# Layer 1 of a two-layer block on Trainium2: the two heads' transposes and value products issued together, output parts split earlier, a third accumulator bank and a moved table load

## The chip, the cores and the metric

The kernel runs on one core of a Trainium2 chip. The time is the device time of one execution in microseconds (us). A core has TensorE (PE, matrix products, with its weight loads shown as PEld), VectorE (DVE), ScalarE (ACT), GpSimd (POOL) and SyncE (SP, which issues most of the DMAs here). Each engine works through its own list of instructions in order, and waits on semaphores for the others.

## What is computed

The reference is a first block (time mixing of eight heads by a recurrence, and eight heads of stick-breaking attention), followed by two layers on 512 tokens of width 1024 with 256 tokens of context: layer 0 with a short convolution and a gated FFN, layer 1 with neighbourhood attention of 16 heads of width 64 and the same kind of FFN. All of it is float32. The change lies in layer 1:

```python
q, k, v = _qkv_heads(h, w_qkv, g_q, g_k)          # q and k normalised per head
qc, kc, vc = _qkv_heads(hc, w_qkv, g_q, g_k)      # of the context
...
s_win = jnp.einsum('bqhd,brkhd->bhqrk', q_r, k_r) * scale + bias[None]
s_ctx = jnp.einsum('bqhd,bchd->bhqc', q_r, kc) * scale
s = jnp.concatenate([s_win.reshape(...), s_ctx], axis=-1)
p = jax.nn.softmax(s, axis=-1)
o = p_win @ v_r + p_ctx @ vc
...
x = x + g1 * (o @ w_out)
h = rms_norm(x, norm_ffn) * (1 + sc2) + sh2
gate, up = jnp.split(h @ w_in, 2, axis=-1)
x = x + g2 * ((silu(gate) * up) @ w_out)
```

## The kernel before, in words

Every float32 operand of a large product is split in two fp32r parts, hi (a cast on ScalarE) and lo (a subtraction on VectorE), and a product is three matmuls (`mm3`, L172 hi by hi, L173 lo by hi, L174 hi by lo). Weights come by DMA into `st` and are split by `split_w` (L155 cast, L156 subtraction) into four pairs of buffers `wh`, `wl` of 512 columns; one weight tile of 1024 columns takes two of them. Names ending in h and l (h0h, h0l) are such parts.

The order on each engine is set by a list scheduler at build time, from priorities and its estimates of durations. `order()` adds a dependency that the scheduler respects and that makes no semaphore.

PSUM banks are asked for by tag: `acc` (two banks), `cacc` (one), `sm` for scores, `pt` for transposes and head norms, `py` for a pair's output.

Layer 1 takes its 16 heads in eight pairs (`na_pair`, p = 0 to 7). A pair projects q and k (`xgemm`, and the context's k in `cacc`), normalises them per head (`hnorm`: L811 square, L298 and L299 block sums of `hsh` and `hsl`, L242 and L249 logarithm and exponential, L818, L819 and L821 the gain) and lays the two heads out in `qh`, `ql` and `kk` (L826, L827; L839, L840). GpSimd subtracts the bias from the mask (`bt`, L846). Then come four blocks of 128 queries, each with two heads e = 0, 1. For one head of one block: scores (L863, L864, two or four matmuls into `sm`), addition of mask and bias with a row minimum on VectorE (L868), exponential with row sum on ScalarE (L870), reciprocal on VectorE (L871), scaling on GpSimd (L872), four transposes of 128 columns in float32 on PE (L876 into `pT`), and a copy out of PSUM (L877, VectorE for e = 0, ScalarE for e = 1). After two blocks `na_values` issues ten value products (L896, five for each head, in float32; the two heads write different halves of the partitions of `py`); these two blocks are called a half here. The projections of the next pair are put by the scheduler between the scores, transposes and value products of this one, so PE has other work while a head's probabilities are made.

A pair's output is copied to a float32 tile `o{k}` (L882 on ScalarE, L883 on VectorE). After the loop over pairs in the program, each is split into `oh` parts (L307, L308), pair 7's straight from PSUM. The output product takes its eight tiles `attn_w_out[m]` one after the other through the two `acc` banks, each with eight steps k over the pairs. In the schedule its first tiles fill PE during pair 7, which has no next pair to project.

Then the FFN's norm: `rsqrt` (L242 logarithm, L249 exponential) and `modulate` (L288 on VectorE, L290 on ScalarE for h..h, L291 on VectorE for h..l), in two halves of 256 tokens. The first FFN tile (`lead`) runs gate and up together by halves; it holds both `acc` banks. The FFN's tile applies tanh to the gate (L643) and multiplies (L644), which frees the gate's bank, then takes up (L649) and splits the result (L307, L308). Tanh needs another set of function tables on ScalarE than logarithm and exponential in this kernel; the load is placed right ahead of the first tanh.

## Time and profile before

| what | value |
|---|---|
| runs | 2081.96, 2076.53, 2077.85 us; median 2077.85 us |
| profiled execution | 2080.14 us, of which the span from first to last instruction is 2078.4 us |
| mean granted TensorE clock | 0.994 |
| layer 1's attention, first score of pair 0 to last value product of pair 7 | 1440.34 to 1665.32 us |
| last matmul of the first FFN tile, first of the second | 1721.36 and 1724.59 us |

In the rows of the profile a group or an instruction is written as line, engine, operation, output <- inputs, partitions times elements. A row of the timeline begins with the start in us from the span's start and the duration; in brackets stands the engine's idle time before it and what ended it. Matmuls are pipelined: one of 512 columns is shown with some 0.39 us, while the next starts some 0.23 us after it, so spacing is read from starts. A clock (PEclk) of 1.00 is the full TensorE clock.

### The profile page before, as it was taken

To read this page: it belongs to the slowest core of one execution; us is meant where nothing else is said; L and a number is where in the kernel's file an instruction comes from. 1 tells how busy PE (TensorE), PEld (TensorE's weight loads), DVE (VectorE), ACT (ScalarE), POOL (GpSimd) and SP (SyncE) were. 2 spreads that over 40 slices of the span, in tenths; PEclk is the share of its full clock that TensorE was granted. 3 is DMA by queue.
4 is the path that set the end of the run, shared out by engine and by line. 5 is a ranking of instruction groups with operands and counts; after the bars stand their busy time and mean duration, and the time that the engine had idled before them with its cause. 6 is when DMAs were issued, how large, how long until landed. Compare 5 with 4: busy or idle time off the path is not lost.

```text
span 2078.4 us, 33492 instructions
## 1 busy us (share of the span) xinstructions
PE 2029.1 (98%) x13564; PEld 1637.2 (79%) x13564; DVE 1230.9 (59%) x2641; ACT 795.6 (38%) x1493; POOL 131.5 (6%) x212
## 2 busy tenths in 40 slices
PE   6999999998999999999999999999999999999999
PEld 3766667666888888888888888898777687888887
DVE  2869888658766738675446343444666754444443
ACT  3536444446322224221222222335776743323232
POOL 0000000000000000000001000001223200000000
PEclk9999999999999999999999999999999999999999
DMA  7432222122233312344235221122111122323323
GB/s 280 150 113 92 94 74 93 40 81 83 92 122 122 122 61 93 131 133 151 94 135 177 72 96 61 58 82 67 56 52 51 36 82 82 101 93 97 98 98 103
DMA packets 61355, 203.59 MB, mean 98 GB/s; under 512 B 6928, under 2 KB 8976, under 8 KB 61200
## 3 DMA queue, kind: packets, MB, share of 16 engines
q1 hardware_dynamic: 45360, 145.77, 21.6%
q0 software_dynamic: 15120, 55.06, 8.1%
q8 instruction: 106, 1.74, 0.4%
q10 hardware_dynamic: 720, 0.62, 0.1%
q14 instruction: 49, 0.40, 0.1%
HBM read 199.32 MB, written 2.10 MB: 97 GB/s over the span
## 4 chain that ended last, share of the span: by engine, by line
PE 87%; ACT 3%; DVE 3%; issue 1%; POOL 0%; DMA 0%; POOLq 0%; DVEq 0%; ACTq 0%
PE acc L173 20%; PE acc L174 20%; PE acc L172 19%; PE cacc L174 5%; PE cacc L173 5%; PE cacc L172 5%; PE py L896 2%; PE pT L876 1%; PE ss L1150 1%; PE so L1172 1%; PE sm L863 1%; PE sm L864 1%; PE G L980 1%; DVE nt L288 1%; PE ss L1165 1%
## 5 line engine op out<-in xcount | busy, mean ns | idle before, releaser
L155 ACT CAST wh<-st 128x512 fp32r<-128x512 f32 (+2 forms) x481 | 292.1, 609 | 722.0 <-PE acc L173 283.2
L156 DVE TENSOR_TENSOR wl<-st,wh 128x512 fp32r<-128x512 f32 (+2 forms) x481 | 323.4, 674 | 350.7 <-ACT wh L155 347.4
L172 PE MATMUL acc<-xzzh,wh 128*128 128x512 f32 x352 | 138.8, 394 | 0.0
L174 PE MATMUL acc<-xzzh,wl 128*128 128x512 f32 x352 | 138.0, 392 | 0.0
L173 PE MATMUL acc<-xzzl,wh 128*128 128x512 f32 x352 | 138.0, 392 | 0.0
L210 DVE CUSTOM_DVE_ANT_0 junk<-ast,cb,vec 128x512 bf16<-128x512 f32 x168 | 125.0, 744 | 15.7 <-DMA ast<-in_w_ada_dram 13.6
L210 DVE CUSTOM_DVE_ANT_0 junk<-ast,cb,m 128x512 bf16<-128x512 f32 x168 | 125.5, 747 | 2.8
L200 POOL DMA_DIRECT2D ast<-in_w_ada_dram x96 | 50.7, 528 | 996.5 <-DVE m L210 887.1
L174 PEld LDWEIGHTS acc<-xzzh,wl 128*128 128x128 f32 x352 | 66.0, 188 | 14.8
L173 PEld LDWEIGHTS acc<-xzzl,wh 128*128 128x128 f32 x352 | 66.1, 188 | 13.5 <-issue 0.5
L172 PEld LDWEIGHTS acc<-xzzh,wh 128*128 128x128 f32 x352 | 66.1, 188 | 13.4 <-issue 0.5
L173 PE MATMUL acc<-h7l,wh 128*128 128x512 f32 (+1 forms) x164 | 65.2, 397 | 4.1 <-DVE h7l L308 4.1
L172 PE MATMUL acc<-h0h,wh 128*128 128x512 f32 (+1 forms) x164 | 65.6, 400 | 3.0 <-DVE fs L644 3.0
L173 PE MATMUL cacc<-czzl,wh 128*128 128x256 f32 x240 | 68.1, 284 | 0.0
L172 PE MATMUL cacc<-czzh,wh 128*128 128x256 f32 x240 | 67.7, 282 | 0.0
L174 PE MATMUL cacc<-czzh,wl 128*128 128x256 f32 x240 | 67.3, 280 | 0.0
L172 PE MATMUL acc<-h3h,wh 128*128 128x512 f32 (+1 forms) x164 | 65.1, 399 | 0.9 <-DVE x L452 0.9
L174 PE MATMUL acc<-h2h,wl 128*128 128x512 f32 (+1 forms) x164 | 65.8, 401 | 0.0
L174 PE MATMUL acc<-h0h,wl 128*128 128x512 f32 (+1 forms) x164 | 65.7, 401 | 0.0
L173 PE MATMUL acc<-h3l,wh 128*128 128x512 f32 (+1 forms) x164 | 65.4, 399 | 0.3 <-DVE h3l L291 0.3
L174 PE MATMUL acc<-h7h,wl 128*128 128x512 f32 (+1 forms) x164 | 65.1, 397 | 0.4 <-issue 0.4
L173 PE MATMUL acc<-h5l,wh 128*128 128x512 f32 (+1 forms) x164 | 65.4, 399 | 0.0
(731 smaller groups left out, 5539.4 us busy)
## 6 DMA issues: line engine op xcount, KB each, us to landing
ast<-in_w_ada_dram POOLq DMA_DIRECT2D x96, 512.0 KB, 3.8
st<-in_ffn_w_in_dram SPq DMA_DIRECT2D x88, 512.0 KB, 3.5
st<-in_ffn_w_out_dram SPq DMA_DIRECT2D x32, 448.0 KB, 3.4
st<-in_w_in_dram SPq DMA_DIRECT2D x24, 512.0 KB, 3.5
st<-in_conv_w_in_dram SPq DMA_DIRECT2D x24, 512.0 KB, 3.5
ast<-in_ada_n_dram SPq DMA_DIRECT2D x16, 512.0 KB, 8.9
st<-in_ffn_w_out_dram SPq DMA_DIRECT2D x16, 512.0 KB, 3.5
st<-in_w_qk_dram SPq DMA_DIRECT2D x16, 512.0 KB, 3.4
```

The lines of the kernel that those rows point to most:

```text
L155: nc.scalar.copy(hi[:, :n], sl)
L156: nc.vector.tensor_tensor(lo[:, :n], sl, hi[:, :n].bitcast(F32), ALU.subtract)
L172: mm(out, lhsT=lh, rhs=rh, start=first, stop=False)
L173: mm(out, lhsT=lh, rhs=rl, start=False, stop=False)
L174: return mm(out, lhsT=ll, rhs=rh, start=False, stop=last)
L200: self.nc.gpsimd.dma_start(st, src)
L210: i = self.nc.vector.tensor_tensor_reduce(out=junk, in0=st[:, hs], in1=c[:, hs], scale=0.5, scalar=o if hf else self.V(bname, j), op0=ALU. ...
L288: nc.vector.scalar_tensor_tensor(t, xs[k], gain[:, k:k + 1], rstd, op0=ALU.mult, op1=ALU.mult)
L863: mm(o, lhsT=qh[:, e, qs], rhs=ks, start=True, stop=False)
L864: mm(o, lhsT=ql[:, e, qs], rhs=ks, start=False, stop=True)
L876: nc.tensor.transpose(pT[:, to], s[:, 128 * i:128 * i + 128], self.C("ident"))
L896: self.nc.tensor.matmul(po[r, cs], lhsT=v[:, r], rhs=pts[e][:, blk:blk + n].rearrange("p a t -> p (a t)"), start=i == 0, stop=i == len(wor ...
```

## The change

- `na_pair` first makes both heads' probabilities of a block, then issues both heads' transposes. The first head's transposes are ordered behind the second head's scaling, and in `na_values` the first head's products behind the last copy of the transposes. Both are orders for the scheduler, without a semaphore. (The second head's scaling is what `ready` names after the loop.)
- The outputs of pairs 0 to 3 are split straight from PSUM into tiles of their own (`o0h`, `o0l` and so on). Those of pairs 4 to 6 are copied as before and split when pair 7 is issued, pair 7's from PSUM.
- The output product's tile m = 2 and the gate of FFN tile i = 1 use the bank `cacc`, which is free by then, in place of `acc`.
- The load of the table set with tanh is placed behind the last exponential of the FFN's norm.

```diff
--- before.py
+++ after.py
@@ -554,8 +554,8 @@
                 nc.sync.dma_start(A["dbg_x0"][k], xs[k])
                 nc.sync.dma_start(A["dbg_c0"][k], self.xc[k])
 
-    def gemm2(self, src, h, hc, k0=0, k1=KT):
-        po = self.psum("acc")
+    def gemm2(self, src, h, hc, k0=0, k1=KT, tag="acc"):
+        po = self.psum(tag)
         w = self.load_w(src[:, k0 * 128:k1 * 128], (k1 - k0) * 128)
         outs = [(po, h)]
         if hc is not None:
@@ -636,7 +636,7 @@
             hid = []
             for i in range(t0, t0 + np_):
                 lead = i == 0 and self.lead((w1[0], w1[NH_T]), *hs, halves=split)
-                pg = lead[0] if lead else self.gemm2(w1[i], *hs)
+                pg = lead[0] if lead else self.gemm2(w1[i], *hs, tag="cacc" if split and i == 1 else "acc")
                 ss = []
                 for (_, _, n, pre, _), ps in zip(st, pg):
                     s = pool.tile([128, n], F32, tag=pre + "cs", name="fs")
@@ -679,8 +679,8 @@
             return pre[t]
         return self.xgemm(W[t], h)
 
-    def xgemm(self, src, h, k0=0, k1=KT):
-        out = self.psum("acc")
+    def xgemm(self, src, h, k0=0, k1=KT, tag="acc"):
+        out = self.psum(tag)
         self.gemm(out, src, dict((k0 + i, t) for i, t in enumerate(h)), k0, k1)
         return out
 
@@ -744,22 +744,27 @@
                 nc.scalar.copy(va[:, 2:4, cs], v2(pvs[1]))
                 for t in range(2):
                     nc.vector.tensor_copy(vc[4 * t + qd], pvs[2][:, 256 * t:256 * t + 256])
-            os = [pool.tile([128, S], F32, name=f"o{k}") for k in range(KT - 1)] + [None]
+            oh = [self.hl(pool, S, f"o{k}") for k in range(4)]
+            os = [pool.tile([128, S], F32, name=f"o{k}") for k in range(4, KT - 1)]
             wp = es.enter_context(self.open(name="naw", bufs=2))
             self.qls = [wp.tile([128, 2, S], F32R, name=f"ql{i}", bufs=1) for i in range(2)]
             for t in self.qls:
                 nc.gpsimd.memset(t[64:128, 0].bitcast(F32), 0.0)
                 nc.gpsimd.memset(t[0:64, 1].bitcast(F32), 0.0)
             for p in range(8):
-                last = self.na_pair(p, W, h, hc, gq, va, vc, mask, bts, os[p], wp)
-            oh = []
-            for k, tag in enumerate(("qh", "kk", "pt0", "pt1") * 2):
-                t = wp.tile([128, 2, S], F32R, tag=tag, name="oh", bufs=2)
-                oh.append((t[:, 0], t[:, 1]))
-                if k < KT - 1:
-                    self.split(oh[k], os[k])
-            for a, b in ((slice(0, 448), slice(64, S)), (slice(448, S), slice(0, 64))):
-                self.split((oh[7][0][:, a], oh[7][1][:, a]), last[:, b])
+                po = self.na_pair(p, W, h, hc, gq, va, vc, mask, bts, wp)
+                if 4 <= p < KT - 1:
+                    nc.scalar.copy(os[p - 4][:, :448], po[:, 64:])
+                    nc.vector.tensor_copy(os[p - 4][:, 448:], po[:, :64])
+                    continue
+                if p == KT - 1:
+                    for k, tag in enumerate(("qh", "kk", "pt0", "qh")):
+                        t = wp.tile([128, 2, S], F32R, tag=tag, name="oh", bufs=2)
+                        oh.append((t[:, 0], t[:, 1]))
+                        if k < 3:
+                            self.split(oh[4 + k], os[k])
+                for a, b in ((slice(0, 448), slice(64, S)), (slice(448, S), slice(0, 64))):
+                    self.split((oh[p][0][:, a], oh[p][1][:, a]), po[:, b])
             sx, late = {"bufs": 4, "acc_tag": "q", "sq_tag": "s"}, []
             rstd = wp.tile([128, S], F32, tag="q", name="rstd")
             hv = [slice(0, 256), slice(256, 512)]
@@ -770,7 +775,7 @@
                 self.stat(m, xs[m], S, wp, "x", sx, c)
 
             for m in range(6):
-                add(m, self.xgemm(A["attn_w_out"][m], oh), slice(0, S))
+                add(m, self.xgemm(A["attn_w_out"][m], oh, tag="cacc" if m == 2 else "acc"), slice(0, S))
             for m in (6, 7):
                 w, po = self.load_w(A["attn_w_out"][m], 1024), self.psum("acc")
                 self.gemm(po[:, hv[0]], None, cut(oh, hv[0]), w=w)
@@ -786,7 +791,8 @@
                 turn(0, range(2 * i, 2 * i + 2))
                 add(m, po, hv[1])
             self.prefetch(A["ffn_w_in1"][0], A["ffn_w_in1"][NH_T])
-            self.rsqrt(rstd[:, hv[1]], sx["ps"][:, hv[1]])
+            done = self.rsqrt(rstd[:, hv[1]], sx["ps"][:, hv[1]])
+            self.order(nc.scalar.preload_act_table_set("exp_and_others"), done)
             turn(0, range(4, KT))
             turn(1, range(KT))
             if self.dbg:
@@ -797,7 +803,7 @@
         for k in range(KT):
             nc.sync.dma_start(A["out"][k], xs[k])
 
-    def na_pair(self, p, W, h, hc, gq, va, vc, mask, bts, oh, wp):
+    def na_pair(self, p, W, h, hc, gq, va, vc, mask, bts, wp):
         nc = self.nc
         TT, STT = nc.vector.tensor_tensor, nc.vector.scalar_tensor_tensor
         mm = nc.tensor.matmul
@@ -850,6 +856,7 @@
             qs = slice(128 * j, 128 * j + 128)
             if j % 2 == 0:
                 pts = [wp.tile([128, 8, 128], F32, tag=f"pt{e}", name=f"pt{e}", bufs=2) for e in range(2)]
+            probs = []
             for e in range(2):
                 ps = self.psum("sm")
                 ke = kk[:, e]
@@ -869,20 +876,21 @@
                                                scalar=3.0e38, op0=ALU.add, op1=ALU.min, accum_out=st[:, 0:1])
                 nc.scalar.activation(s, s, AF.Exp, scale=-1.0, bias=st[:, 0:1], accum_out=st[:, 1:2])
                 nc.vector.reciprocal(st[:, 2:3], st[:, 1:2])
-                nc.gpsimd.tensor_scalar(s, s, st[:, 2:3], 1.0, op0=ALU.mult, op1=ALU.mult)
+                ready = nc.gpsimd.tensor_scalar(s, s, st[:, 2:3], 1.0, op0=ALU.mult, op1=ALU.mult)
+                probs.append(s)
+            for e, s in enumerate(probs):
                 pT = self.psum("pt", (128, 4, 128), "pT")
                 for i in range(4):
                     to = 1 - i if j == 3 and i < 2 else i
-                    nc.tensor.transpose(pT[:, to], s[:, 128 * i:128 * i + 128], self.C("ident"))
-                (nc.scalar.copy if e else nc.vector.tensor_copy)(pts[e][:, j % 2::2], pT)
+                    t = nc.tensor.transpose(pT[:, to], s[:, 128 * i:128 * i + 128], self.C("ident"))
+                    if e == 0:
+                        self.order(t, ready)
+                copied = (nc.scalar.copy if e else nc.vector.tensor_copy)(pts[e][:, j % 2::2], pT)
             if j % 2:
-                self.na_values(p, j // 2, po, pts, va, vc)
-        if oh is None:
-            return po
-        nc.scalar.copy(oh[:, :448], po[:, 64:])
-        nc.vector.tensor_copy(oh[:, 448:], po[:, :64])
-
-    def na_values(self, p, half, po, pts, va, vc):
+                self.na_values(p, j // 2, po, pts, va, vc, copied)
+        return po
+
+    def na_values(self, p, half, po, pts, va, vc, ready):
         c0 = 256 * half
         near = va[:, :, 128 * p:128 * p + 128]
         far = [vc[4 * n + p // 2][:, 128 * (p % 2):128 * (p % 2) + 128] for n in range(2)]
@@ -893,9 +901,11 @@
             for e in range(2):
                 r = slice(64 * e, 64 * e + 64)
                 cs = slice(c0 + 128 * col, c0 + 128 * (col + n))
-                self.nc.tensor.matmul(po[r, cs], lhsT=v[:, r],
-                                      rhs=pts[e][:, blk:blk + n].rearrange("p a t -> p (a t)"),
-                                      start=i == 0, stop=i == len(work) - 1)
+                o = self.nc.tensor.matmul(po[r, cs], lhsT=v[:, r],
+                                          rhs=pts[e][:, blk:blk + n].rearrange("p a t -> p (a t)"),
+                                          start=i == 0, stop=i == len(work) - 1)
+                if e == 0:
+                    self.order(o, ready)
 
     def mix(self, ps, mu, omu, out):
         nc = self.nc
```

What follows are the lists of instructions at three places, of the kernel before with its line numbers, then of the changed one with its own (L885 are the transposes there, L904 the value products, L870 and L871 the scores).

TensorE, pair 3, second half: the end of its two blocks, of the kernel before. `pt_15125` is the first head, `pt_15126` the second.

```order
L174 MATMUL acc<-h3h,wl 128x512
L896 MATMUL py<-pt_15125,vc_13272 64x256
L172 MATMUL acc<-h4h,wh 128x512
L173 MATMUL acc<-h4l,wh 128x512
L876 MATMUL pT<-con,s 128x128 x4
L298 MATMUL pt<-hsh,b64r 128x512
L299 MATMUL pt<-hsl,b64r 128x512
L174 MATMUL acc<-h4h,wl 128x512
L172 MATMUL acc<-h5h,wh 128x512
L896 MATMUL py<-pt_15126,vc_13272 64x256
L896 MATMUL py<-pt_15125,vc_13276 64x256
L896 MATMUL py<-pt_15126,vc_13276 64x256
```

The same place in the changed kernel, from the transposes of the half's first block on (`pt_15135` first head, `pt_15136` second):

```order
L885 MATMUL pT<-con,s 128x128 x8
L173 MATMUL acc<-h4l,wh 128x512
L174 MATMUL acc<-h4h,wl 128x512
L885 MATMUL pT<-con,s 128x128 x8
L172 MATMUL acc<-h5h,wh 128x512
L173 MATMUL acc<-h5l,wh 128x512
L904 MATMUL py<-pt_15135,vc_13272 64x256
L904 MATMUL py<-pt_15136,vc_13272 64x256
L904 MATMUL py<-pt_15135,vc_13276 64x256
L904 MATMUL py<-pt_15136,vc_13276 64x256
```

The lone product of the first head and the projection matmuls and transposes behind it are gone from between the value products; transposes stand in groups of eight, and the ten value products (four of them shown) in one row.

TensorE ahead of pair 7's first scores, of the kernel before (`oh` are split outputs, `hsh` and `hsl` the norm of pair 7's k):

```order
L298 MATMUL pt<-hsh,b64r 128x512
L172 MATMUL acc<-oh,wh 128x512
L299 MATMUL pt<-hsl,b64r 128x512
L173 MATMUL acc<-oh,wh 128x512
L174 MATMUL acc<-oh,wl 128x512
L298 MATMUL pt<-hsh,b64r 128x256
L299 MATMUL pt<-hsl,b64r 128x256
L172 MATMUL acc<-oh,wh 128x512
L173 MATMUL acc<-oh,wh 128x512
L174 MATMUL acc<-oh,wl 128x512
L863 MATMUL sm<-kk,qh 128x256
L864 MATMUL sm<-kk,ql_13954 128x256
```

The same place in the changed kernel; 22 of the output product's matmuls, which begin with `acc<-o0h`, stand ahead of these:

```order
L173 MATMUL acc<-o2l,wh 128x512
L174 MATMUL acc<-o2h,wl 128x512
L172 MATMUL acc<-o3h,wh 128x512
L173 MATMUL acc<-o3l,wh 128x512
L174 MATMUL acc<-o3h,wl 128x512
L172 MATMUL acc<-oh,wh 128x512
L173 MATMUL acc<-oh,wh 128x512
L174 MATMUL acc<-oh,wl 128x512
L172 MATMUL cacc<-o0h,wh 128x512
L870 MATMUL sm<-kk,qh 128x256
L871 MATMUL sm<-kk,ql_13958 128x256
```

Six matmuls of the output product stood ahead of the first score; now 31 do, the last of them in the bank `cacc`.

ScalarE at the end of the first FFN tile, of the kernel before (`fs` is the tile of the tanh):

```order
L290 ACTIVATE h5h<-nt,m_1_71 128x256
L155 CAST wh<-st 128x512 x2
L290 ACTIVATE h6h<-nt,m_1_71 128x256
L290 ACTIVATE h7h<-nt,m_1_71 128x256
L155 CAST wh<-st 128x512
L643 ACT_TABLE_LOAD
L643 ACTIVATE fs<-acc 128x512
```

ScalarE behind the exponential of the FFN's norm in the changed kernel:

```order
L242 ACTIVATE rstd<-sm,epsb 128x256
L249 ACTIVATE rstd<-rstd 128x256
L795 ACT_TABLE_LOAD
L290 ACTIVATE h4h<-nt,m_1_71 128x256
L290 ACTIVATE h5h<-nt,m_1_71 128x256
L290 ACTIVATE h6h<-nt,m_1_71 128x256
```

The load has moved from ahead of the tanh to ahead of the casts h4h to h7h of the first half of the tokens.

## The prediction

> **What bounds the kernel now.** I read the page first, then the view of waits, then windows and the timeline of the places that the change touches. The page says that TensorE (PE) sets the time:
>
> ```profile
> PE 2029.1 (98%) x13564; PEld 1637.2 (79%) x13564; DVE 1230.9 (59%) x2641; ACT 795.6 (38%) x1493; POOL 131.5 (6%) x212
> ...
> PE 87%; ACT 3%; DVE 3%; issue 1%; POOL 0%; DMA 0%; POOLq 0%; DVEq 0%; ACTq 0%
> ```
>
> PE is busy 98% of the span and has 87% of the chain that ended last. A change that takes no matmul away can only win what PE loses: time in which it stands still, time between starts that its own switches of operation cost, and time at a lower clock. What it stands still for, from layer 1 on, is the view of waits with PE's own rows:
>
> ```profile
> PE acc L172 <- DVE fs L644: 3.0, 1, 3.0
> PE sm L863 <- DVE kk L840: 1.9, 1, 1.9
> ...
> PE pT L876 <- POOL s L872: 1.4, 3, 0.7
> ```
>
> Two single waits are most of it: 3.0 us at the start of the FFN and 1.9 us ahead of pair 7's first scores. The transposes (L876) lose 1.4 us in three waits for GpSimd. The windows show the rest. Columns are length, then busy time and count of PE, PEld, DVE, ACT and POOL, PE clock, DMA share and GB/s:
>
> ```profile
> 1440.34:1457.10 16.76, 16.68 (x115) 12.41 (x115) 10.98 (x31) 10.26 (x23) 7.95 (x10) 1.00 0.20 62
> 1528.82:1547.10 18.28, 18.23 (x119) 13.07 (x119) 12.15 (x33) 11.26 (x25) 8.02 (x10) 1.00 0.18 58
> 1451.95:1457.10 5.15, 5.15 (x42) 4.06 (x41) 2.29 (x4) 2.18 (x4) 2.22 (x3) 1.00 0.31 95
> 1539.67:1547.10 7.43, 7.43 (x47) 4.91 (x46) 4.12 (x8) 4.21 (x8) 2.41 (x3) 1.00 0.23 71
> 1646.80:1650.20 3.40, 2.87 (x11) 2.68 (x12) 2.73 (x5) 1.78 (x4) 0.00 (x0) 0.50 0.00 0
> 1725.30:1728.70 3.40, 3.40 (x9) 2.64 (x9) 1.04 (x2) 0.62 (x1) 0.00 (x0) 0.50 0.50 154
> 1710.35:1720.46 10.11, 10.02 (x78) 9.44 (x77) 10.11 (x27) 7.07 (x16) 0.00 (x0) 1.00 0.22 72
> ```
>
> The first two rows are pairs 0 and 3, from the first score to the end of the last value product, the next two their second halves; PE has hardly an idle moment there, so what can be won is in the spacing. The two windows at clock 0.50 lie right behind the two long waits.
>
> **Part 1: the attention order, pairs 0 to 6.** Nothing is removed; transposes and value products are put together. The trace of before holds both orders, since pair 0's second half already runs as all pairs shall: eight transposes, two projection matmuls, eight, two, ten value products.
>
> ```profile
> 1451.95 1.09 PE L876 MATMUL pT<-con,s 128*128 128x128 f32 x8
> 1452.79 0.48 PE L174 MATMUL acc<-h2h,wl 128*128 128x512 f32 x1
> 1453.11 0.40 PE L172 MATMUL acc<-h3h,wh 128*128 128x512 f32 x1
> 1453.48 1.07 PE L876 MATMUL pT<-con,s 128*128 128x128 f32 x8
> ...
> 1454.94 1.14 PE L896 MATMUL py<-pt,vc 128*64 128x256 f32 x7
> ```
>
> It takes 5.15 us (1451.95 to 1457.10) with 4 matmuls of 512 columns in it. Pair 3's second half is split up:
>
> ```profile
> 1541.90 0.40 PE L173 MATMUL acc<-h3l,wh 128*128 128x512 f32 x1
> 1542.14 0.40 PE L174 MATMUL acc<-h3h,wl 128*128 128x512 f32 x1
> 1542.46 0.65 PE L896 MATMUL py<-pt,vc 128*64 128x256 f32 x2
> 1543.04 0.49 PE L172 MATMUL acc<-h4h,wh 128*128 128x512 f32 x1
> 1543.38 0.40 PE L173 MATMUL acc<-h4l,wh 128*128 128x512 f32 x1
> ```
>
> Matmuls of 512 columns start 0.23 to 0.24 us apart (1541.90, 1542.14). The lone first value product costs 0.09 to enter, 0.58 to the next start, and 0.11 behind that (1543.04 to 1543.38): 0.78; taking it out of the ten saves only some 0.06 there, so about **0.7 us for each lone product**. As a check, the whole half takes 7.43 us with 12 matmuls of 512 columns (2.76 us at 0.23) and two transposes fewer (about 0.2), so 4.9 net, against 5.15 - 0.92 = 4.2 net in pair 0: again 0.7.
>
> Second halves: pairs 2 to 6 change, 5 of them, at 0.4 to 0.7 each (0.4 is the difference of whole pairs: the timeline counts 19 matmuls of other products in pair 3, from 1529.39 to 1544.91, and 14 in pair 0, from 1440.92 to 1454.62; less 0.227 for each, 18.28 leaves 14.0 and 16.76 leaves 13.6); I take 0.55, **-2.8**.
>
> First halves: all seven lose a lone product (-0.7) and one or two entries into transposes at about 0.14 (1453.11 to 1453.48, less 0.23), but get new waits. The second head's four transposes now stand right behind the first's, and both wait for GpSimd's scaling:
>
> ```profile
> L872 POOL TENSOR_SCALAR s<-s,st 128x512 f32<-128x512 f32 x64 | 45.6, 720 | 211.6 <-DVE st L871 200.5 <-PE sm L864 5.4 <-PE pT L876 4.2
> ```
>
> Two scalings end 0.72 apart at best, and four transposes take 0.42 (eight from 1451.95 to 1452.79: 0.84), so each group of eight in the scores' part waits 0.3; two groups make 0.6. Queued behind such a wait on PE are the scores of the next block, then the value products. I take -0.85 + 0.6 = -0.25 each: **-1.8**. Bounds: +0.5 each (the second head a whole exponential late in both groups) and -0.85 (no wait), +3.5 to -6.
>
> Between pairs, the ScalarE and VectorE chain from a pair's end to the next pair's first score (hsq, hsh, k, kk) now has to fit beside a shorter PE stretch, and for pairs 0 to 3 two casts and two subtractions of the output halves (L307, L308) replace two copies. PE's cover here is the next pair's projections. ScalarE is busy 11.3 of 18.3 us, so most of it hides; I put 0.15 to each pair, **+1.0** (0 to +2.5). The longest single wait for L872, 0.7 in the row above, lies in pair 5 and goes with the regrouping: **-0.6**. Sum of part 1: -2.8 - 1.8 + 1.0 - 0.6 = **-4.2**, bounds -10 to +3.
>
> **Part 2: early split and third bank, pair 7.** What stands ahead of pair 7's scores:
>
> ```profile
> 1642.11 0.40 PE L174 MATMUL acc<-oh,wl 128*128 128x512 f32 x1
> ...
> 1645.00 0.40 PE L174 MATMUL acc<-oh,wl 128*128 128x512 f32 x1
> 1647.33 0.58 PE L863 MATMUL sm<-kk,qh 128*128 128x256 f32 x1 [1.93 <-DVE kk L840]
> ```
>
> From 1642.11 to 1647.33 are 5.22 us for six matmuls (four of 512 columns, two of 256), about 1.15 us of work: 4.1 us lost, since of the output product only part k=0 was split. With four parts split early and a third bank, 31 of its matmuls stand ahead of those scores in place of 6; 25 more at 0.227 are 5.7 us, enough for 4.1. Nothing of this work is new: it is done earlier, and PE is the bound behind pair 7 too. What can be late next is kk, with two or three weight casts (L155, some 0.5 each) ahead of it on ScalarE, and the third tile's weights, whose buffers come free only when the first tile's matmuls are done; I leave 0.7 (0 to 2.5). The clock of 0.50 behind the wait costs half of the 2.9 us that PE worked in that window, 1.45. Pair 7's own grouping, as a late pair: -0.4. Sum: -3.4 - 1.45 - 0.4 = **-5.2** (-6 to -2).
>
> **Part 3: FFN start, third bank and table load.**
>
> ```profile
> 1721.36 0.28 PE L174 MATMUL acc<-h7h,wl 128*128 128x256 f32 x1
> 1721.84 1.28 ACT L643 ACT_TABLE_LOAD   x1
> 1723.13 0.60 ACT L643 ACTIVATE fs<-acc 128x512 f32<-128x512 f32 x1
> ...
> 1724.59 0.47 PE L172 MATMUL acc<-h0h,wh 128*128 128x512 f32 x1 [2.96 <-DVE fs L644]
> ```
>
> PE's idle time is 2.96 here, and 3.12 by starts (from 1721.36, and half of 0.23 for 256 columns). The window at 0.50 behind it did 3.4 us of work at half speed, 1.7. With another bank the second tile needs no bank from L644 and can follow at once; its first weights were cast before the lead ended. Gross: -3.1 - 1.7 = -4.8. The load's new place is not free:
>
> ```profile
> 1711.04 0.42 ACT L249 ACTIVATE rstd<-rstd 128x256 f32<-128x256 f32 x1
> 1711.36 0.49 ACT L290 ACTIVATE h4h<-nt,m 128x256 fp32r<-128x256 f32 x1
> ...
> 1719.06 0.68 DVE L156 TENSOR_TENSOR wl<-st,wh 128x512 fp32r<-128x512 f32 x1
> 1719.66 0.47 DVE L291 SCALAR_TENSOR_TENSOR h6l<-nt,m,h6h 128x256 fp32r<-128x256 f32 x1
> ```
>
> It goes between these two ScalarE rows and moves h4h by 1.28; VectorE's h4l is queued in order behind it, and VectorE is the lead's second limit: in the window 1710.35 to 1720.46 it is busy 10.11 of 10.11 us, so 1.28 lost at its head is lost at the lead's end. The new order also puts two weight subtractions (0.6 each) ahead of h7l where one stood ahead of h6l: +0.6. Price 1.9, between 0 if the lead's slack takes it all and 3.2 if twice the load is lost. Its idle time is spread over the lead, so I expect no half clock. Sum: **-2.9** (-4.8 to -1.6).
>
> The Trainium skill ("ScalarE: Activation LUTs", What ACT_TABLE_LOAD costs) puts a switch of tables at about 1283 ns of load and 1380 ns of drain. The trace has the 1.28, and 0.01 between its end and the tanh, so the drain is not seen; by the page the new place would cost 1.4 more, part 3 -1.5 and the time 2067.0.
>
> **Sum.** -4.2 - 5.2 - 2.9 = -12.3 against the profiled execution's 2080.1 (span 2078.4): 2067.8. That execution lies 2.3 above the median of the runs, 2077.85; against the median I forecast 2065.6, in round numbers **2066 us** (-0.6%).
>
> **Rivals.** *The new waits eat the attention gain.* For: the groups of eight wait for the slower of two heads, in all eight pairs, and GpSimd also runs the bias subtraction between them. Against: pair 0's second half shows no wait in this order. Part 1 at +2 in place of -4.2: 2072.
>
> *The table load costs more in its new place*: the lead's last part ends 3.2 us late in place of 1.9, as the two weight subtractions ahead of h7l wait for buffers: part 3 at -1.6, 2066.9, inside the range.
>
> *The moved product is not ready*: the third tile's weights or kk come late and pair 7 keeps its wait and half clock. For: four weight buffers serve three tiles. Against: 30 of the 31 matmuls need only the first two tiles' weights. Part 2 at -1: 2070.
>
> *Slower: the clock falls in the transposes.* After a 3.4 us window of which PE was idle for most, the next ran at 0.50. If transposes and value products count as idle, the stretches of eight, two, eight, two, ten would be such windows; the price is 1.7 us each, two in each of eight pairs, 27 us: 2093. It decides from the point at which some 3 us pass with one or two projection matmuls. Against: pair 0's second half is such a stretch, at clock 1.00.
>
> The Trainium skill ("TensorE: Matmul & The Clock Gate", Part 4: PE-mode transpose) says that transposes do not count as busy for the clock in the same way; that row of pair 0 speaks against any effect here.
>
> **How the numbers follow.** A measurement of this kernel can tell about 0.3%, 6.2 us, from no change: faster is below 2071.6. Forecast (2059 to 2071) 0.60; waits 0.20 (0.05 of it below 2071.6); table load 0.08, faster; product late 0.07 (0.06 faster); clock 0.05, slower. So faster 0.79, same 0.16, slower 0.05. The range takes the forecast with the bounds that do not all fall together, and the waits' case up to part 1's +3: 2059 to 2074.
>
> **What would show it.** Right: no lone L896 rows in pairs 0 to 6 and pair 3's length below 18.0; PE's gap ahead of pair 7's first score under 1 us, and the clock at 1.00 there; the second FFN tile starting within 0.2 us of the lead's end, the table load ahead of h4h, and the lead's end 1 to 2 us later after the norm's exponential than the 10.3 of before (1711.04 to 1721.36). Wrong: waits of PE for L872 well above 5 us in sum; half clock inside the pairs; a gap behind the lead though the bank is free (weights).

## The result, and the profile after

The changed kernel takes 2060.84 us (median of 4 runs, 2058.45 to 2062.35) against 2079.15 us (4 runs): a ratio of 0.9911, 95% interval 0.9893 to 0.9929. That is 18 us, where 12 were forecast. (One more run of the kernel before, in the last series, took 2803.69 us at a mean granted clock of 0.653, and no comparison here uses it.) The profiled execution took 2062.35 us, its span is 2060.6; the one of before took 2080.14, so the two profiles differ by 17.8.

The page after, busy time and the chain that ended last:

```profile
PE 2016.6 (98%) x13564; PEld 1635.1 (79%) x13564; DVE 1233.7 (60%) x2641; ACT 795.1 (39%) x1493; POOL 129.9 (6%) x212
...
PE 87%; ACT 3%; DVE 2%; issue 1%; POOL 0%; DMA 0%; ACTq 0%; DVEq 0%; POOLq 0%
```

As many matmuls as before, and PE as busy in per cent: the gain does not show in shares. It shows in PE's waits from layer 1 on (total, times, longest):

```profile
PE pt L298 <- ACT hsh L296: 2.9, 7, 0.5
PE acc L172 <- ACT h4h L290: 1.3, 1, 1.3
PE sm L282 <- ACT sq L274: 1.1, 1, 1.1
PE pT L885 <- POOL s L879: 0.7, 3, 0.2
```

The 3.0 us for `fs` and the 1.9 for `kk` are gone. New is 1.3 for h4h, behind the moved table load. The transposes' wait for GpSimd, which was to grow, has fallen from 1.4 to 0.7 in this view; the starts further down say otherwise. The windows, columns as before the change; the first row is pair 3, the next two its halves, the last two the stretch ahead of pair 7 and most of the FFN's first two tiles:

```profile
1526.41:1541.93 15.52, 15.28 (x114) 12.24 (x113) 11.63 (x31) 10.03 (x23) 7.99 (x10) 1.00 0.18 54
1526.41:1536.67 10.26, 10.03 (x74) 8.10 (x74) 8.72 (x27) 7.62 (x19) 4.76 (x7) 1.00 0.15 53
1536.67:1541.93 5.26, 5.26 (x42) 4.15 (x40) 2.92 (x4) 2.41 (x6) 3.23 (x4) 1.00 0.24 58
1627.00:1641.18 14.18, 13.71 (x71) 11.27 (x71) 8.56 (x15) 12.10 (x22) 0.00 (x0) 1.00 0.10 38
...
1695.68:1715.78 20.10, 18.78 (x122) 16.88 (x121) 16.43 (x36) 12.48 (x25) 0.00 (x0) 1.00 0.28 99
```

The clock is 1.00 in all of them. Pair 3 is 15.5 us long, though with six other matmuls fewer inside it, which now stand between the pairs; so lengths alone mislead. A fair measure takes what the matmuls of a stretch need from it. I call **lost time** the time from start to start less the spacing that the same matmul has in a steady row: 0.2265 us for 512 columns, 0.1185 for 256, 0.109 for a transpose, 0.108 and 0.0545 for one pass of a value product of 256 and 128 columns. Worked out from the starts of all PE instructions, by stretch (the first half of a pair runs to the end of its first ten value products):

```
lost time of PE, us          before   after   difference   forecast
first halves, pairs 0 to 6    13.06    7.18     -5.88        -1.8
second halves, pairs 0 to 6    9.55    6.23     -3.32        -3.4
between pairs 0 to 6           4.32    6.15     +1.83        +1.0
ahead of pair 7                4.69    1.13     -3.56  \
pair 7                         4.78    2.56     -2.22  /     -5.2
output product                 1.87    1.89     +0.02         0
FFN norm and first two tiles   6.19    2.43     -3.76        -2.9
sum                           44.46   27.57    -16.89       -12.3
```

(The forecast for second halves has the wait of pair 5 in it.) The other 0.9 us of the 17.8 lie ahead of layer 1's attention, where both kernels run the same instructions. There one kernel's executions differ: in the runs below, the first score starts between 1437.1 and 1442.6 us. Single times of these runs therefore carry some 3 us that say nothing of the change, while the lost time of one stretch comes out alike within 0.1 us wherever the order and the clock are the same. So the experiments are read by lost time.

Pair 3 in the changed kernel, TensorE's timeline:

```profile
1530.86 0.60 PE L885 MATMUL pT<-con,s 128*128 128x128 f32 x4
1531.21 0.36 PE L870 MATMUL sm<-kk,qh 128*128 128x256 f32 x1
1531.81 0.66 PE L885 MATMUL pT<-con,s 128*128 128x128 f32 x4 [0.23 <-POOL s L879]
...
1533.33 0.60 PE L885 MATMUL pT<-con,s 128*128 128x128 f32 x4
1533.68 0.48 PE L870 MATMUL sm<-kk,qh 128*128 128x512 f32 x1
...
1534.46 0.40 PE L871 MATMUL sm<-kk,ql 128*128 128x512 f32 x1
1534.79 1.08 PE L904 MATMUL py<-pt,vc 128*64 128x256 f32 x8
1535.70 1.04 PE L904 MATMUL py<-pt,va 128*64 128x256 f32 x12
1536.67 1.31 PE L885 MATMUL pT<-con,s 128*128 128x128 f32 x8
```

Four score matmuls stand between the last transposes (1533.33) and the value products (1534.79), which run in one go in 1.88 us. The row at 1531.81 shows a wait of 0.23 for GpSimd, but idle time is not all of it. In the first block of every half of pairs 0 to 6 the second head's transposes start 0.05 to 0.06 us behind the end of their scaling, in pair 3 at 1531.81 and 1537.33:

```profile
1531.06 0.69 POOL L879 TENSOR_SCALAR s<-s,st 128x512 f32<-128x512 f32 x1 [0.83 <-DVE st L878]
...
1536.57 0.70 POOL L879 TENSOR_SCALAR s<-s,st 128x512 f32<-128x512 f32 x1
...
1537.33 0.66 PE L885 MATMUL pT<-con,s 128*128 128x128 f32 x4
```

The eight transposes of the last PE row above begin at 1536.67, and their second four 0.66 later, where four take 0.44 in a steady row. No idle time is shown for that, since the end of a matmul is modelled. By starts PE loses 0.26 to 0.48 us there in each first half and 0.16 to 0.28 in each second half: the wait for the slower head has come. What has been won against it stands in the value products, as the lost time on the two sides of each half's first value product shows:

```
lost time of PE, pairs 0 to 6, us          before   after   e_nothint
first halves, up to the value products       6.3     6.2      5.9
first halves, from there on                  6.8     1.1      5.2
second halves, up to the value products      2.4     3.3      2.4
second halves, from there on                 7.2     3.0      3.0
```

(e_nothint is an experiment further down; 0.7 of the 7.2 is pair 5's wait.) Ahead of pair 7 no wait for `kk` is left: matmuls of the output product run up to the first score.

```profile
1640.73 0.39 PE L174 MATMUL acc<-oh,wl 128*128 128x512 f32 x1
1640.95 0.39 PE L172 MATMUL cacc<-o0h,wh 128*128 128x512 f32 x1
1641.18 0.28 PE L870 MATMUL sm<-kk,qh 128*128 128x256 f32 x1
```

In the FFN's first tile the stall stands where the load now is, and the second tile's first three matmuls even run ahead of the first tile's last four:

```profile
1697.72 0.28 PE L174 MATMUL acc<-h3h,wl 128*128 128x256 f32 x1
1699.30 0.50 PE L172 MATMUL acc<-h4h,wh 128*128 128x256 f32 x2 [1.30 <-ACT h4h L290]
...
1707.77 0.40 PE L172 MATMUL acc<-h7h,wh 128*128 128x256 f32 x2
1708.01 0.40 PE L172 MATMUL cacc<-h0h,wh 128*128 128x512 f32 x1
...
1708.71 0.28 PE L173 MATMUL acc<-h7l,wh 128*128 128x256 f32 x1
```

### The profile page after: what moved, and what is told of

It is laid out like the page before. It is cut to its first block, busy times and chain, and to the rows that moved or that the text cites. A ratio compares the mean times of both kernels' runs of the same rounds, so it can differ in the third digit from the quotient of the medians.

```text
span 2060.6 us, 33474 instructions
## 1 busy us (share of the span) xinstructions
PE 2016.6 (98%) x13564; PEld 1635.1 (79%) x13564; DVE 1233.7 (60%) x2641; ACT 795.1 (39%) x1493; POOL 129.9 (6%) x212
## 4 chain that ended last, share of the span: by engine, by line
PE 87%; ACT 3%; DVE 2%; issue 1%; POOL 0%; DMA 0%; ACTq 0%; DVEq 0%; POOLq 0%
PE acc L173 20%; PE acc L174 20%; PE acc L172 20%; PE cacc L174 5%; PE cacc L173 5%; PE cacc L172 5%; PE py L904 2%; PE pT L885 1%; PE ss L1160 1%; PE so L1182 1%; PE sm L870 1%; PE sm L871 1%; PE G L990 1%; PE ss L1175 1%; PE py L1092 1%
## 5 line engine op out<-in xcount | busy, mean ns | idle before, releaser
L172 PE MATMUL acc<-h4h,wh 128*128 128x512 f32 (+1 forms) x163 | 64.5, 398 | 1.3 <-ACT h4h L290 1.3
L173 PE MATMUL acc<-h4l,wh 128*128 128x512 f32 (+1 forms) x163 | 65.3, 401 | 0.0
```

What stands on the lines that cost most here:

```text
L172: mm(out, lhsT=lh, rhs=rh, start=first, stop=False)
L173: mm(out, lhsT=lh, rhs=rl, start=False, stop=False)
```

## The experiments

In the tables the columns are the lost time of the stretches above.

```
lost time, us     first  second  between  ahead   pair   output  FFN    sum
                  halves halves  pairs    of 7    7      product start
before            13.06   9.55    4.32    4.69    4.78    1.87   6.19   44.46
after              7.18   6.23    6.15    1.13    2.56    1.89   2.43   27.57
e_group            7.27   6.17    6.39    5.43    5.05    1.90   4.59   36.80
e_rest            11.48   8.04    5.55    0.97    2.14    1.91   2.43   32.52
e_vhint           10.97   5.95    6.24    1.07    2.57    1.87   2.43   31.10
e_nothint         11.05   5.35    5.98    1.17    2.53    1.90   2.43   30.41
e_notable          7.08   6.23    6.25    1.19    2.53    1.87   1.08   26.23
e_tlate            7.13   6.26    6.26    1.18    2.52    1.88   1.30   26.53
e_nobank           7.16   6.27    6.24    1.19    2.51    1.88   5.07   30.32
e_nosplit          7.26   6.15    6.38    5.42    3.54    1.89   2.43   33.07
e_nom2             7.05   6.25    6.30    1.15    2.87    3.46   2.42   29.50
notable5           7.09   6.24    6.27    1.19    2.51    1.92   1.07   26.29
```

### Part 1 alone, and all but part 1

e_group keeps the new `na_pair` and takes the rest back:

```diff
-            oh = [self.hl(pool, S, f"o{k}") for k in range(4)]
+            os = [pool.tile([128, S], F32, name=f"o{k}") for k in range(KT - 1)] + [None]
...
-                add(m, self.xgemm(A["attn_w_out"][m], oh, tag="cacc" if m == 2 else "acc"), slice(0, S))
+                add(m, self.xgemm(A["attn_w_out"][m], oh, tag="acc"), slice(0, S))
...
-            self.order(nc.scalar.preload_act_table_set("exp_and_others"), done)
```

> Part 1 alone: both heads' probabilities first, transposes and value products ordered together; outputs copied and split as before, banks and table load as before. Theory A (parts add up): pairs 0 to 6 gain what the changed kernel gained there, first halves 5.9, second halves 3.3, given back between pairs 1.8, so about 7.4 us less than before, near 2072; the wait of 3.0 at the FFN and the half clock behind it stay, and so does a wait of 1 to 2 us ahead of pair 7. Theory B (the gain inside the pairs comes from the parts split early, which take copies and splits off the end of a pair): first halves as before (1.8 us of lost time each), time within 3 us of before.

Measured: 2070.2 us beside 2076.3 of the kernel before on the same chip; 7.7 less lost than before. First halves 7.27 and second halves 6.17, as in the changed kernel: for the attention, theory A holds. That the total meets the forecast of 7.4 is in part luck. The attention gives 7.1, ahead of pair 7 and in it 1.0 more is lost than before, and the FFN's start loses 1.6 less, since the half clock that was to stay there did not come. The waits at pair 7 and at the FFN are there again:

```profile
PE pt L298 <- ACT hsh L296: 4.4, 8, 1.8
PE acc L172 <- DVE fs L644: 3.0, 1, 3.0
PE pT L882 <- POOL s L876: 1.2, 4, 0.5
```

One wait for `hsh` is 1.8 us now, which fits shorter pairs that only bring PE to pair 7's chain sooner; no run tests that. The clock falls there for two windows of 3.4 us. At the FFN, PE stood idle 2.96 us as in the kernel before, and yet went on at full clock (second row):

```profile
1636.20:1643.00 6.80, 5.92 (x21) 4.72 (x20) 5.63 (x12) 3.88 (x7) 0.30 (x1) 0.50 0.26 77
...
1716.24:1719.64 3.40, 3.40 (x15) 2.81 (x16) 1.75 (x3) 1.16 (x2) 0.00 (x0) 1.00 0.43 152
```

e_rest is the other way round, the changed kernel with the attention code of before:

```diff
-            probs = []
             for e in range(2):
...
-            for e, s in enumerate(probs):
                 pT = self.psum("pt", (128, 4, 128), "pT")
```

> All but part 1: attention in the code of before, outputs split early, third bank twice, table load moved. Theory A: pair 7 gains 4 to 5.8 and the FFN 3.8, so 8 to 9.5 us less than before, near 2071; halves that keep their lone value product lose 1.8 (first) and 1.45 (second) as before. Theory B: first halves lose about 1.0 without the regrouping, time near 2064.

Measured: 2065.0 us, 11.9 less lost than before; ahead of pair 7, pair 7 and FFN 10.1 of it. The total is between the two theories, and the reason lies in the schedule: with other instructions around it, the scheduler put halves of pairs 1, 2, 4 and 7 in another order by itself. Halves that kept the lone product lost 1.7 to 2.1 (first) and 1.46 (second, pairs 3, 5 and 6), as before; first halves of pairs 1 and 2, without one, 1.21 and 0.93. So an order is what counts, by half, and the same source text can give either.

### What in the first halves was won

e_vhint leaves each head's transposes behind its own probabilities and orders only the value products:

```diff
-            for e, s in enumerate(probs):
-                pT = self.psum("pt", (128, 4, 128), "pT")
+                pT = self.psum("pt", (128, 4, 128), "pT")
...
-                    if e == 0:
-                        self.order(t, ready)
```

> The changed kernel with the transposes left as before (each head's behind its own probabilities), and only the value products ordered behind the last copy. Where this order has ten value products together but transposes in three or four groups of four, the lone product alone is taken away. If the lone product is most of the first halves' gain (0.7 of 0.85), those first halves lose 1.0 to 1.2 us; if the groups of eight are most of it, they lose 1.5 to 1.8.

Measured: 2066.28 us. The first halves of pairs 0, 4 and 6 kept their lone product and lost 2.02 to 2.09. Pairs 1, 2, 3 and 5 have the ten value products together and four groups of four transposes. Pairs 1 and 2 lost 1.25 and 0.93, as in the changed kernel (1.19 and 0.96); pairs 3 and 5 lost 1.33 and 1.35, against 1.82 before and 1.00 after. These two lie between the ranges of the forecast. So grouping the transposes is not what wins in the first halves. Pair 3's timeline shows why it is not 1.0:

```profile
1534.27 0.60 PE L882 MATMUL pT<-con,s 128*128 128x128 f32 x4
...
1535.16 0.40 PE L870 MATMUL sm<-kk,ql 128*128 128x512 f32 x1
1535.34 0.57 ACT L883 COPY pt<-pT 128x512 f32<-128x512 f32 x1
1535.48 1.34 PE L899 MATMUL py<-pt,vc 128*64 128x256 f32 x7
...
1537.84 1.10 PE L882 MATMUL pT<-con,s 128*128 128x128 f32 x8
```

The value products take 2.36 us (1535.48 to 1537.84) in place of 1.88: they begin 1.21 us behind the last transposes, 1.46 in the changed kernel, with three score matmuls between in place of four. That is 0.48, more than all of the difference. The second head's transposes are copied out of `pT` by ScalarE (the ACT row), and that copy ends at 1535.91; the second head's first product starts at 1535.96. From 1535.48 until then the first head's products run alone. How long they do so goes with the value products' lost time wherever the ten stand together: 0.15 us where both heads start at once (first halves of the changed kernel, and pairs 1 and 2 here), 0.42 where the first is alone for 0.28 (second halves), 0.62 here. So taking the lone product and the two stray transposes away is worth the 0.84 that pair 3 won in its value products (0.99 to 0.15), but only if the last transposes and their copies stand early enough; else a part of it comes back.

e_nothint takes only the order of the transposes away:

```diff
                     t = nc.tensor.transpose(pT[:, to], s[:, 128 * i:128 * i + 128], self.C("ident"))
-                    if e == 0:
-                        self.order(t, ready)
```

> The changed kernel without the order of the first head's transposes behind the second head's scaling; the value products keep theirs. The program's order then has more groups of four in the scores. If a group of four more costs 0.1 to 0.15 for its entry, first halves lose 0.2 to 0.4 more than in the changed kernel, second halves about the same, and the time is 1 to 3 us more than the changed kernel's. If the groups of eight cost a wait for the slower head (0.3 each, as the prediction had it), it is up to 2 us less.

Measured: 2.8 us more lost than in the changed kernel, 3.9 in first halves (0.55 each, more than the 0.2 to 0.4 expected), and 0.9 less in second halves. In pairs 2, 4 and 5 a lone product came back (1.70 to 1.87 lost); the four pairs without one lost 1.33 to 1.54. The time agrees with the first of the two forecasts, but not by its reason, the price of an entry. The third column of the table by halves shows it: up to the value products this kernel loses less than the changed one, 5.9 in place of 6.2 and 2.4 in place of 3.3, so holding the first head's transposes back does cost a wait. It loses 4.1 more in the first halves' value products, by the lone products and by late copies (0.61 in each pair without a lone product, as in e_vhint, in place of 0.15).

### The FFN start: bank and table load

e_notable drops the moved load; the compiler puts it ahead of the tanh again:

```diff
-            done = self.rsqrt(rstd[:, hv[1]], sx["ps"][:, hv[1]])
-            self.order(nc.scalar.preload_act_table_set("exp_and_others"), done)
+            self.rsqrt(rstd[:, hv[1]], sx["ps"][:, hv[1]])
```

> The changed kernel with the table load where it was, ahead of the first tanh. Theory C (the third bank alone takes the tanh off PE's path): the stall of 1.40 us inside the first FFN tile goes, the second tile still follows at once, and load, tanh and product (2.6 us) hide behind its 24 matmuls (5.4 us): 1.2 to 1.5 us less than the changed kernel from the norm to the third tile. Theory D (both are needed): a gap of 1 us or more opens at the second or third tile, and the time is the same or more.

Measured: 1.08 lost in place of 2.43. Theory C holds: moving the load costs 1.35 us and wins nothing once the bank is there. ScalarE in this kernel:

```profile
1709.94 1.28 ACT L643 ACT_TABLE_LOAD   x1
1711.24 0.60 ACT L643 ACTIVATE fs<-acc 128x512 f32<-128x512 f32 x1
```

The second tile's gate started at 1707.94 and its up product follows at 1714.60 without a gap. The load ends at 1711.22 and the product that frees the bank (L644) at 1712.56, two microseconds before the bank is needed.

e_tlate puts the load behind the first half's four casts:

```diff
-            self.order(nc.scalar.preload_act_table_set("exp_and_others"), done)
-            turn(0, range(4, KT))
+            done = turn(0, range(4, KT))
+            self.order(nc.scalar.preload_act_table_set("exp_and_others"), done)
             turn(1, range(KT))
```

> The changed kernel with the table load one step later, behind the four casts of the first half of the tokens, where ScalarE stood idle 0.97 us in the trace of before. Theory C: the stall of 1.40 falls to 0.4 or less, 1.0 to 1.4 us less than the changed kernel. If the load delays the second half's casts by all of its 1.28, and VectorE behind it, nothing is won.

Measured: 1.30 lost, 1.13 less than the changed kernel and 0.22 more than e_notable: most of the load falls in ScalarE's idle time there.

e_nobank keeps the load where the change put it and gives the second tile its old bank:

```diff
-                pg = lead[0] if lead else self.gemm2(w1[i], *hs, tag="cacc" if split and i == 1 else "acc")
+                pg = lead[0] if lead else self.gemm2(w1[i], *hs, tag="acc")
```

> The changed kernel with the second FFN tile's gate in the bank it had before; the table load stays moved. PE then waits for cast, tanh and product behind the first tile, 1.7 to 2.0 us. If the clock falls behind any idle time of that size, another 1.7 follows at half clock; if it takes a longer one (3.1 us before), none does. So 1.9 or 3.6 us more than the changed kernel.

Measured: 2.64 more lost. Two of its PE waits, then the window at that place and the one behind it:

```profile
PE acc L172 <- DVE fs L644: 1.8, 1, 1.8
...
PE acc L173 <- DVE h7l L291: 0.4, 1, 0.4
```

```profile
1709.00:1712.40 3.40, 1.39 (x10) 0.98 (x8) 2.27 (x5) 1.62 (x3) 0.00 (x0) 1.00 0.47 147
1712.40:1715.80 3.40, 3.27 (x14) 2.74 (x15) 1.88 (x3) 1.05 (x2) 0.00 (x0) 1.00 0.48 157
```

The wait of 1.8 us comes back, and 0.4 for h7l, which the second tile's matmuls hid; no half clock follows. Against the kernel before, this one loses 1.1 less (6.19 to 5.07). But 1.6 of the 6.19 is half clock, and e_group, with load and bank as before, had none and lost 4.59. Against e_group the moved load without the bank costs 0.5; with the bank it costs 1.35.

### Pair 7: early split and third bank

e_nosplit copies all outputs and splits them when all pairs are done in program order; e_nom2 gives the third tile its old bank (`tag="acc"` for every m):

```diff
-            oh = [self.hl(pool, S, f"o{k}") for k in range(4)]
+            os = [pool.tile([128, S], F32, name=f"o{k}") for k in range(KT - 1)] + [None]
...
-                    self.split((oh[p][0][:, a], oh[p][1][:, a]), po[:, b])
+                self.split((oh[7][0][:, a], oh[7][1][:, a]), last[:, b])
```

> The changed kernel with all eight outputs copied and split as before, when pair 7 is done in program order; attention order and banks of the change stay. If the early split is what fills PE ahead of pair 7, the 3.6 us lost there and 1.2 of the half clock come back, 4 to 5.5 us more than the changed kernel; between pairs 0 to 3 nothing changes by more than 0.2 each. If the third bank alone fills it, under 1 us more.

Measured: 5.5 more lost, 4.3 of it ahead of pair 7 and 1.0 in it; pairs 0 to 6 within 0.3 in all. The waits are back, and the half clock, as the window at 0.50 ahead of pair 7 shows:

```profile
PE pt L298 <- ACT hsh L296: 4.3, 8, 1.8
...
PE sm L868 <- DVE kk L844: 0.5, 1, 0.5
```

```profile
1635.00:1638.40 3.40, 3.29 (x6) 1.78 (x6) 3.06 (x6) 3.05 (x6) 0.00 (x0) 0.50 0.00 0
```

> The changed kernel with the output product's third tile in the bank it had before. Of the 31 matmuls ahead of pair 7's scores only one stood in the third bank, so if the early split does the work there, PE's lost time ahead of pair 7 stays at 1.1 to 1.4 us; inside pair 7, where the third tile gave 8 more matmuls to fill with, 0.3 to 1.5 us more are lost. If the bank is needed, the wait ahead of pair 7 comes back by over 1 us.

Measured: ahead of pair 7 1.15 as in the changed kernel, inside it 0.31 more, as expected. Not foreseen: 1.57 more behind pair 7. With two banks PE has too little left there while the last output is split:

```profile
PE acc L172 <- ACT oh L307: 0.6, 1, 0.6
...
PE acc L172 <- DVE xn L774: 0.4, 1, 0.4
```

So the split fills PE ahead of pair 7; the bank keeps it from waiting behind it.

### The best version

> The changed kernel with the table load at its old place once more, timed in rounds: its lost time of TensorE was 1.3 us below the changed kernel's, so about 2059.5 where the changed kernel has 2060.8, a ratio to the kernel before of 0.990 to 0.991. Executions of one kernel differ by more than 1.3 us, so the rounds can show the step against the kernel before, not the 1.3.

Measured: 2061.89 us (5 runs, 2058.31 to 2062.26) against 2078.0 (median of eight runs of the kernel before), a ratio of 0.9918, 95% interval 0.9903 to 0.9933. It is the kernel of e_notable, and its lost time, 26.29, is the same again and 1.3 less than the changed kernel's. The rounds don't tell it from the changed kernel (0.9893 to 0.9929): the 1.3 us are shown by the traces only.

## Why the prediction was right, and where it was too small

The direction and the places were right: three stretches, each with a gain, and no gain elsewhere. 2066 was too high by 5 us, inside the range.

- *Part 1, second halves.* -3.4 with pair 5's wait; measured -3.3. The half of pair 0 that already ran in the new order was a sound measure: pairs 2 to 6 lose 0.87 to 0.99 there now, pair 0 lost 0.77. The difference is a new wait for the scaling that I had put at nothing, 0.16 to 0.28 in all seven; pairs 0 and 1, which had the order already, lose 0.1 more for it.
- *Part 1, first halves.* Here the step failed: "two groups make 0.6" of new wait for GpSimd in each pair, -0.25 left of 0.85. Measured -0.84 each. The wait itself came, but at one group of a half in place of two: 0.26 to 0.48 by starts at the first, 0.02 to 0.10 at the second. As much was saved beside it: up to the value products the seven first halves lose 6.2 us now and lost 6.3 before. All the gain stands in the value products, 6.8 to 1.1, or 0.82 each where I had 0.7 for the lone product, since in first halves both heads' products now start at once. That -0.84 meets the bound I had set for no wait is luck. The rival that the new waits eat the gain falls all the same: in the second halves the stretch with the wait took back 0.9 of the 4.2 us won behind it, in the first halves nothing.
- *Between the pairs.* +1.0 forecast, +1.8 measured. The place was named: the wait for `hsh` rose from 1.6 us in four waits to 2.9 in seven (one of them ahead of pair 7 in both kernels, 0.6 and 0.5).
- *Part 2.* -5.2 forecast, -5.8 measured: 3.6 ahead of pair 7, where the half clock had not yet begun, and 2.2 in it with the half clock. The 0.7 left for a late `kk` or late weights was not needed; no wait for either is in the list. e_nosplit and e_nom2 show that the split does the work ahead of the scores, and the bank behind the pair (a use I had not counted). The rival of the product that is not ready falls. Pair 7's own grouping, -0.4 in the sum, won nothing at the value products (0.93 and 0.20 lost in its halves before, 0.93 and 0.42 now; its first half kept a lone product).
- *Part 3.* -2.9 forecast, -3.8 measured. The wait of 3.1 is gone and so is the half clock; the stall at the load's new place is 1.46 (1697.72 to 1699.30, less 0.12). But I had counted the half clock, 1.7, as a fixed part of the wait, and e_group kept the wait without it (4.59 lost). Against that the change wins 2.2 at the FFN; the rest of the 3.8 hangs on a half clock that one execution of the kernel before had, and how often it has it no run shows. The 0.6 for a second weight subtraction ahead of h7l did not come: VectorE does both in 1.28 us at 1706.81, and PE fills that time with the second tile, whose bank is free. I had taken the lead's end as the second tile's start; the schedule mixes the two.
- *The drain* of some 1.4 us that the Trainium skill ("ScalarE: Activation LUTs", What ACT_TABLE_LOAD costs) puts behind a load is not seen at the new place either: the load takes 1.28 us and h4h starts 0.02 later (1697.44 to 1698.74).
- *The clock in the transposes.* This window of the changed kernel, columns as above, answers the rival of 2093:

```profile
1430.00:1720.00 290.00, 284.33 (x1774) 232.29 (x1773) 194.55 (x430) 200.78 (x403) 61.54 (x78) 1.00 0.18 60
```

All of the attention, the output product and the FFN's start at 1.00, with eight pairs of dense transposes and value products. What the Trainium skill ("TensorE: Matmul & The Clock Gate", Part 4: PE-mode transpose) says of transposes and the clock shows no effect here.

## What to carry to other kernels

Where the bound engine is busy 98%, look at its starts and take the steady spacing off: here 44 us of such lost time stood in some 300 us, half of it inside the attention's pairs, where the engine was hardly ever idle by the view of waits. Starts also show short waits that this view leaves out. An order hint that holds back the first of two equal things until the second is ready did make a wait here; it was small, and the hint paid two steps later, where both heads' copies were done before their products began. So price a hint over the whole chain, and read its gain there too. When two remedies are made for one wait (a free bank, and a load moved off the path), try each alone: the second cost 1.35 us beside the first, and 0.5 without it.

## What the runs showed of the hardware

Half clock came behind stretches of idle PE shorter than one window of 3.41 us, but not behind all of them. It followed 1.93 us of idle time with 0.47 ahead of it (before, pair 7) and 2.96 (before, FFN), but not the same 2.96 in e_group, nor 1.77 (e_nobank) or 1.30 (after). What fits all of them is how much of the idle time falls in one step of 3.41 us, counted on from the half clock windows of the same trace. From 600 us on, four steps of the twelve traces were idle for 1.63 to 2.69 us, and half clock followed each; none followed a step idle for 1.52 or less, but for one of e_group that ran at half clock itself (0.88). The 2.96 us lay with 2.69 in one step in the kernel before, and with 1.44 and 1.52 in two steps in e_group. This was read from the traces afterwards, and no run tests it.

The two windows of before at 0.50 cost about 1.45 us (half of the busy time in the first) and 1.6 (6.19 lost at the FFN against 4.59 in e_group). In the first block, ahead of everything that was changed, such windows came and went between executions of the same instructions; e_nobank, for one, had a stretch at 0.50 from 308.5 to 318.8 us that neither the kernel before nor the changed one has. So a single time could not settle a step of one or two microseconds, while lost time by stretch did, to 0.1 where the clock was 1.00.

Value products of one head took as long alone as beside the other head's. In the changed kernel's pair 3, passes of 128 columns of one head alone started 0.11 us apart (1541.51, 1541.62, 1541.73), and pairs of them, one of each head, 0.11 apart too (1536.13, 1536.24, 1536.35). So the lost time of the value products rises with the time for which one head runs alone.
